# Weight sums laid out one at a time, the gate product on VectorE, and the embedding's rows in the squares' tiles

## The chip, the cores and the metric

The kernel runs on one NeuronCore of one Trainium2 chip. The metric is the device time of one execution in microseconds; the time before is the median of three runs. A profile of one further execution was taken. In it PE is TensorE's matmul (PEld its weight load), DVE is VectorE, ACT is ScalarE, POOL is GpSimd and SP is SyncE, whose queue issues the DMAs.

## The reference

Two layers over 512 tokens of width 1024, float32. Each layer is

```python
h = h + 0.5 * swiglu(rmsnorm(h, ffn1_norm[i]), ffn1_w_gu[i], ffn1_w_down[i])
h = h + mixer(rmsnorm(h, mix_norm[i]))       # layer 0: state-space scan, layer 1: neighbourhood attention
h = h + 0.5 * swiglu(rmsnorm(h, ffn2_norm[i]), ffn2_w_gu[i], ffn2_w_down[i])
gate = sigmoid(rmsnorm(h, ple_norm[i]) @ ple_w_gate[i])
h = h + gate * rmsnorm(p[i] @ ple_w_proj[i], ple_post_norm[i])

def swiglu(x, w_gu, w_down):                 # hidden width 2816 = 22 tiles of 128
    g, u = jnp.split(x @ w_gu, 2, axis=-1)
    return (jax.nn.silu(g) * u) @ w_down
```

The change touches the four `swiglu` (two in each layer) and the product `p[i] @ ple_w_proj[i]`, with `p[i]` 512 x 256 (the embedding's rows).

## The kernel before

**Layout and precision.** The state `h` lies in eight tiles of 128 features x 512 tokens. Every operand of a matmul is split in a high half (a cast) and a low half (the rest). A `gemm` therefore issues three matmuls for each tile of the contraction: high x high (L251), high x low (L254), low x high (L255). For weights the high half `wh` is cast on ACT (L209) and the low half `wl` is subtracted on DVE (L211); for activations these are L269 and L270. There are three buffers each of `wh` and `wl`, four of raw weights `wr`, 24 wide tiles `md`, four tiles `sq` for squares, seven `t`.

**An FFN.** Of the 22 hidden tiles the first six ("plain", `gate_up`) take two units of 24 matmuls each. The other 16 go in eight pairs. In a pair, gate and up rows by halves of the features make a 2 x 2 matrix of weight quadrants `a11`, `a12`, `a21`, `a22`, and the activations one of feature halves by token halves. Their product is formed by seven block products instead of eight (`block`, 24 matmuls 128x256 each, L466 to L468), from sums of quadrants on both sides. The weight sums are `s1 = a21 + a22` (L227), `s2 = s1 - a11` (L228), `a11 - a21` (L229, written over `a21`) and, after block 1, `a12 - s2` (L234). Block 0 uses `a11` as it is, block 1 uses `s2`, block 2 what is in `a21`, block 3 uses `s1`, block 4 `a12`, block 5 the fourth sum, block 6 `a22`. `a21` and `a11` are loaded into `wr`, `a22` and `a12` into `md`.

After a block DVE adds its PSUM to what is kept (L472); ACT copies that of block 0 (L476) and takes silu (L490, L494). After blocks 5 and 6 comes the gate product on POOL (L502), and `halve` splits the result on ACT (L507) and DVE (L508).

**The order.** `ffn_order` lists plain tiles, blocks and downs. A "down" is the down projection of one of the eight `h` tiles over a chunk of hidden tiles: six in the first chunk (18 matmuls), four in the others (12 matmuls). Its result is added on DVE (L527). Downs of the chunk before stand after blocks 0, 2, 4 and 6 of each pair. In the second FFN of a layer `ple_proj` (the product with the embedding's rows, "between") stands ahead of the last chunk's downs. `plan` turns that into a list of steps for weights, which `prep_next` works off at most three units ahead of PE: "u" loads and splits a unit, "g" takes the four quadrants of a pair and issues the three sums, "o" splits a block's operand. `loads` is the order of DMAs on SP's queue. A scheduler then orders the instructions of each engine by what they depend on and by their place in the program, so their order on an engine is not that of the code.

Of the kernel before, what the change touches and what calls it, by code (L numbers as in the profile page):

```python
# [48 lines left out]
def ffn_order():  # L49

    for f in range(PLAIN):
        yield "plain", f
    for c in range(1, len(CHUNKS)):
        a, b = CHUNKS[c]
        blocks = [(p, i) for p in range(a // 2, b // 2) for i in range(7)]
        d = 0
        for n, (p, i) in enumerate(blocks):
            yield "block", p, i  # L60
            while d < KD and (d + 0.5) * len(blocks) <= KD * (n + 1):
                yield "down", c - 1, d
                d += 1
    yield "between",
    for d in range(KD):
        yield "down", len(CHUNKS) - 1, d
# [3 lines left out]
def trunk(ctx, tc, A, out):  # L70
# [72 lines left out]
    def plan():  # L143


        for i in range(stop):
            l, w = divmod(i, 4)
            if w in (0, 2):
                gu, gw, dn = [A[f"w_{x}{1 + w // 2}"][l] for x in ("gu", "gw", "dn")]
                for what, *a in ffn_order():  # L150
                    if what == "plain":
                        for x in range(2):
                            yield "u", gu[a[0], x]
                    elif what == "block":
                        p, i_ = a
                        if i_ == 0:
                            yield "g", [gw[p - PLAIN // 2, x, y] for x, y in ((1, 0), (0, 0), (1, 1), (0, 1))]
                        yield "o", i_
                    elif what == "down":
                        b = CHUNKS[a[0]]  # L160
                        yield "u", dn[a[1], :, b[0] * P:b[1] * P]
                    elif w == 2:
                        for n in range(2):
                            yield "u", A["w_proj"][l, n]
            elif w == 3:
                for n in range(KD):
# [12 lines left out]

    todo = list(plan())  # L180

    loads = [x for what, a in todo if what != "o"
             for x in (zip(a, ("wr", "wr", "md", "md")) if what == "g" else [(a, "wr")])]
    todo = iter(todo)
    raws, ready, splits, blocks = [], [], [], {}
    waiting = {"wr": 0, "md": 0}

    def load_unit():
# [25 lines left out]
    def wide():  # L214
        return md().rearrange("p a b -> p (a b)")

    def prep_next():
        item = next(todo, None)
        if item is None:
            return False  # L220
        what, a = item
        if what == "u":
            split_raw(*take())
        elif what == "g":
            a21, a11, a22, a12 = [take()[0] for _ in range(4)]
            s1, s2 = wide(), wide()
            v.tensor_add(out=s1, in0=a21, in1=a22)  # L227
            v.tensor_sub(out=s2, in0=s1, in1=a11)  # L228
            v.tensor_sub(out=a21, in0=a11, in1=a21)  # L229
            blocks.update({0: a11, 1: s2, 2: a21, 3: s1, 4: a12, 5: s2, 6: a22})  # L230
        else:
            split_raw(blocks[a], 1024)
            if a == 1:
                v.tensor_sub(out=blocks[5], in0=blocks[4], in1=blocks[5])  # L234
        top_up()
        return True

# [118 lines left out]
            return self.ss.end()  # L356


    def ffn(norm, nxt, between=lambda: None, first=None):
        R = [None]  # L360
        mids = {}

# [94 lines left out]
        def block(p, i):  # L457

            pt = mm_bank()
            hi, lo = unit()  # L460
            for j in range(2):
                for kk in range(4):
                    sl = slice((4 * j + kk) * P, (4 * j + kk + 1) * P)
                    o = pt[:, j * HT:(j + 1) * HT]
                    xh, xl = xs[i][kk]
                    te.matmul(out=o, lhsT=hi[:, sl], rhs=xh, start=j == 0 and kk == 0, stop=False)  # L466
                    te.matmul(out=o, lhsT=hi[:, sl], rhs=xl, start=False, stop=False)  # L467
                    te.matmul(out=o, lhsT=lo[:, sl], rhs=xh, start=False, stop=j == 1 and kk == 3)  # L468
            k = kept

            def add(to, other):
                v.tensor_add(out=k[to], in0=pt, in1=k[other])  # L472

            if i == 0:
                k["s"] = t2()
                s.copy(out=k["s"], in_=pt)  # L476
            elif i == 1:
                k["u"] = t2()
                add("u", "s")
            elif i == 2:  # L480
                k["v"] = t2()
                add("v", "u")
            elif i == 3:
                k["w"] = t2()
                add("w", "v")
                add("u", "u")
            elif i == 4:

                add("s", "s")
                s.activation(out=k["s"], in_=k["s"], func=AF.Silu)  # L490
            else:
                if i == 5:
                    add("u", "u")
                    s.activation(out=k["u"], in_=k["u"], func=AF.Silu)  # L494
                    x, gate, c = k["w"], k["u"], slice(HT, T)
                    k["hl"] = md(F32R), md(F32R)
                    for j in range(2):
                        mids[2 * p + j] = tuple(y[:, j, :] for y in k["hl"])
                else:
                    add("v", "v")  # L500
                    x, gate, c = k["v"], k["s"], slice(0, HT)
                g.tensor_mul(out=x, in0=x, in1=gate)  # L502
                halve(k["hl"], x, c)

        def halve(hl, x, c):
# [5 lines left out]
        for what, *a in ffn_order():  # L511
            if what == "plain":
                gate_up(a[0])
                while left and R[0] is not None:
                    sums(left.pop(0))
                    if a[0] < 4:
                        break
            elif what == "block":
                block(*a)
            elif what == "between":  # L520
                made = between()
            else:
                c, d = a
                last = c == len(CHUNKS) - 1
                pt = mm_bank() if last else px_bank()
                gemm(pt, unit(), [mids[f] for f in range(*CHUNKS[c])])
                v.scalar_tensor_tensor(out=h[d], in0=pt, scalar=0.5, in1=h[d], op0=ALU.mult, op1=ALU.add)  # L527
                if last:
                    nxt(d)
                    if d == 2 and made is not None:  # L530
                        made[1]()
# [1 line left out]


    def ple_proj(l):
        pt_ = xa(F32)
        sy.dma_start(out=pt_, in_=A["p"][l])
        prs = []
        for k in range(2):
            pr = xa()  # L540
            split(pr, pt_[:, k, :], None)
            prs.append(pr)
        ss = SumSq()
        pp = []
# [12 lines left out]

        def finish():
            r3 = ss.rsqrt(4.0, 4.0 * EPS)
            for n in range(KD):  # L560
                pp[n] = (pp[n], r3)

        return pp, finish

    def ple(l, norm, pp, nxt):
        halves = (slice(0, T // 2), slice(T // 2, T))
# [697 lines left out]
    for i in range(stop):  # L1264
        l, w = divmod(i, 4)
        last = i == stop - 1
        m = None if last else Norm(gains[i + 1], (lambda: md(F32R)) if w == 2 else xa)
        nxt = done if last else m.prep
        if w == 0:
            ffn(n, nxt, first=first if i == 0 else None)  # L1270
        elif w == 1:
            (ssd if l % 2 == 0 else attention)(n, nxt)
        elif w == 2:
            pp = ffn(n, nxt, lambda: ple_proj(l))
        else:
            ple(l, n, pp, nxt)
        n = m
# [99 lines left out]
```

## Time and profile before

| | us |
|---|---|
| median of three runs | 2443.38 (2441.11 to 2443.71) |
| profiled execution, device time | 2437.86 |
| its span in the trace | 2436.1 |
| PE busy | 2354.6 (97%) |
| DVE busy | 1799.9 (74%) |
| ACT busy | 1107.4 (45%) |
| POOL busy | 481.0 (20%) |

The mean granted clock of TensorE was 0.99 of full speed. A row of a group reads: line, engine, operation, output <- inputs, shapes, count, then busy us and mean ns of one, then the idle time of the engine just before them and what ended it. A row of a timeline reads: start, duration (us), engine, line, operation, and in brackets the idle time before it with its releaser. The pairs of the four FFNs lie at about 77 to 360, 1006 to 1285, 1440 to 1722 and 2062 to 2346 us.

### The profile page before, as it was taken

The numbers are of one execution on the slowest core, as the hardware profiler recorded it, in microseconds if no ns is written. First come the engines' busy times: TensorE is split into PE (matmuls) and PEld (weight loads), VectorE is DVE, ScalarE is ACT, GpSimd is POOL, SyncE is SP. The second block draws the span as 40 slices with busy tenths as digits, with TensorE's granted clock in tenths as the row PEclk, the third lists the DMA queues.
The fourth block names the chain that finished last, engine by engine and source line by source line (L and its number), as shares of the span: only waits on it lengthen the run. The fifth ranks groups of instructions, "written<-read, shape, count | busy, mean of one in ns | idle before, by whom it ended". The sixth has DMA issues, their size and how long they took to land. (4 is left out here: it accounts for less than half of the span.)

```text
span 2436.1 us, 35198 instructions
## 1 busy us (share of the span) xinstructions
PE 2354.6 (97%) x13810; PEld 2036.8 (84%) x13810; DVE 1799.9 (74%) x2501; ACT 1107.4 (45%) x1819; POOL 481.0 (20%) x373
## 2 busy tenths in 40 slices
PE   9999999999999999999999999999999999999998
PEld 8888888888888888888887888888877888988887
DVE  7777768877777757877676887677678758677757
ACT  5433335655556744433335443333437644333343
POOL 1101111344545631111103211011100011011120
PEclk9999999999999999999999999999999999999999
DMA  5223314544444543332223232222442323333222
GB/s 184 91 88 104 100 53 139 174 136 143 142 141 130 166 150 96 102 106 89 93 70 104 87 118 91 96 83 74 147 134 100 113 84 116 92 95 100 68 81 85
DMA packets 98950, 265.95 MB, mean 109 GB/s; under 512 B 11984, under 2 KB 12880, under 8 KB 98784
## 3 DMA queue, kind: packets, MB, share of 16 engines
q1 hardware_dynamic: 98496, 263.57, 33.8%
q8 instruction: 108, 1.77, 0.3%
q14 instruction: 58, 0.48, 0.1%
q10 hardware_dynamic: 288, 0.14, 0.0%
HBM read 253.40 MB, written 10.26 MB: 108 GB/s over the span
## 5 line engine op out<-in xcount | busy, mean ns | idle before, releaser
L255 PE MATMUL ps<-md,wl 128*128 128x512 f32 x2128 | 841.7, 396 | 56.7 <-DVE wl L211 56.7
L251 PE MATMUL ps<-md,wh 128*128 128x512 f32 x2128 | 846.7, 399 | 8.5 <-ACT md L269 8.0
L254 PE MATMUL ps<-md,wh 128*128 128x512 f32 x2128 | 838.5, 394 | 2.3 <-DVE md L270 1.6
L209 ACT CAST wh<-wr 128x1024 fp32r<-128x1024 f32 (+2 forms) x401 | 357.6, 893 | 454.8 <-PE ps L254 210.6
L255 PEld LDWEIGHTS ps<-md,wl 128*128 128x128 f32 x2128 | 404.4, 190 | 155.4 <-DVE wl L211 70.6
L211 DVE TENSOR_TENSOR wl<-wr,wh 128x1024 fp32r<-128x1024 f32 (+2 forms) x401 | 427.9, 1067 | 116.4 <-ACT wh L209 90.9
L251 PEld LDWEIGHTS ps<-md,wh 128*128 128x128 f32 x2128 | 404.9, 190 | 91.8 <-ACT md L269 10.0
L254 PEld LDWEIGHTS ps<-md,wh 128*128 128x128 f32 x2128 | 405.1, 190 | 85.3 <-issue 3.3
L502 POOL TENSOR_TENSOR t<-t,t 128x512 f32<-128x512 f32 x64 | 124.3, 1942 | 974.0 <-ACT t L494 876.3
L209 ACT CAST wh<-md 128x1024 fp32r<-128x1024 f32 x160 | 167.4, 1046 | 275.0 <-PE ps L467 263.3
L472 DVE TENSOR_TENSOR t<-ps,t 128x512 f32<-128x512 f32 x224 | 151.7, 689 | 157.5 <-PE ps L468 157.5
L468 PE MATMUL ps<-sc,wl 128*128 128x256 f32 x896 | 254.0, 284 | 2.2 <-DVE wl L211 2.2
L466 PE MATMUL ps<-sc,wh 128*128 128x256 f32 x896 | 253.8, 283 | 1.6 <-ACT wh L209 1.6
L467 PE MATMUL ps<-sc,wh 128*128 128x256 f32 x896 | 254.0, 284 | 0.0
L468 PE MATMUL ps<-md,wl 128*128 128x256 f32 x896 | 253.6, 283 | 0.0
L467 PE MATMUL ps<-md,wh 128*128 128x256 f32 x896 | 253.5, 283 | 0.0
L466 PE MATMUL ps<-md,wh 128*128 128x256 f32 x896 | 253.4, 283 | 0.0
L211 DVE TENSOR_TENSOR wl<-md,wh 128x1024 fp32r<-128x1024 f32 x160 | 195.2, 1220 | 25.7 <-ACT wh L209 25.7
L297 POOL TENSOR_TENSOR sq<-sq,sq 128x512 f32<-128x512 f32 x71 | 100.9, 1421 | 425.9 <-ACT sq L293 425.1
L466 PEld LDWEIGHTS ps<-sc,wh 128*128 128x128 f32 x896 | 172.4, 192 | 6.0 <-ACT wh L209 2.0
L467 PEld LDWEIGHTS ps<-sc,wh 128*128 128x128 f32 x896 | 172.2, 192 | 3.9
L468 PEld LDWEIGHTS ps<-sc,wl 128*128 128x128 f32 x896 | 172.1, 192 | 2.4 <-DVE wl L211 2.4
(207 smaller groups left out, 3024.2 us busy)
## 6 DMA issues: line engine op xcount, KB each, us to landing
wr<-in_w_in_dram SPq DMA_DIRECT2D x65, 512.0 KB, 3.6
wr<-in_w_gw_dram SPq DMA_DIRECT2D x64, 512.0 KB, 3.5
md<-in_w_gw_dram SPq DMA_DIRECT2D x64, 512.0 KB, 5.2
wr<-in_w_dn_dram SPq DMA_DIRECT2D x128, 256.0 KB, 2.7
wr<-in_w_gu_dram SPq DMA_DIRECT2D x44, 512.0 KB, 3.4
hs<-crow SPq DMA_DIRECT2D x64, 256.0 KB, 3.9
wr<-in_w_dn_dram SPq DMA_DIRECT2D x32, 384.0 KB, 3.2
wr<-in_w_qkv_dram SPq DMA_DIRECT2D x24, 512.0 KB, 3.6
```

Source lines behind the costliest of these rows:

```text
L209: splits.append(s.copy(out=hi[:, :n], in_=raw[:, :n]))
L211: v.tensor_sub(out=lo[:, :n], in0=raw[:, :n], in1=hi[:, :n])
L251: m = te.matmul(out=pt, lhsT=hi[:, sl], rhs=part(xp, 0, cols), start=first and k == 0, stop=False)
L254: te.matmul(out=pt, lhsT=hi[:, sl], rhs=part(xp, 1, cols), start=False, stop=False)
L255: te.matmul(out=pt, lhsT=lo[:, sl], rhs=part(xp, 0, cols), start=False, stop=last and k == n - 1)
L297: (v if fast else g).tensor_add(out=self.acc, in0=self.acc, in1=q)
L466: te.matmul(out=o, lhsT=hi[:, sl], rhs=xh, start=j == 0 and kk == 0, stop=False)
L467: te.matmul(out=o, lhsT=hi[:, sl], rhs=xl, start=False, stop=False)
L468: te.matmul(out=o, lhsT=lo[:, sl], rhs=xh, start=False, stop=j == 1 and kk == 3)
L472: v.tensor_add(out=k[to], in0=pt, in1=k[other])
L502: g.tensor_mul(out=x, in0=x, in1=gate)
```

## The change

Three things, each seen in the diff:

1. The step "g" only takes the quadrants. The three sums become steps "s" of their own. They and the group's loads are listed beside blocks 4, 5 and 6 of the pair before (for the first pair: beside the last three plain units). What the blocks use is kept for each pair.
2. The gate product is issued on `v` (DVE) and not on `g` (POOL).
3. The embedding's rows are loaded by two DMAs of 256 KB into two `sq` tiles ahead of the last chunk's first block, and not by one of 512 KB into an `md` tile at "between"; `ple_proj` becomes a generator for that.

```diff
+                def ahead(p, i_):
+                    if i_ == 0:
+                        yield "g", [gw[p - PLAIN // 2, x, y] for x, y in ((1, 0), (0, 0), (1, 1), (0, 1))]
+                    yield "s", (p, i_)
+
                 for what, *a in ffn_order():
                     if what == "plain":
                         for x in range(2):
                             yield "u", gu[a[0], x]
+                            n = 2 * a[0] + x - (2 * PLAIN - 3)
+                            if n >= 0:
+                                yield from ahead(PLAIN // 2, n)
                     elif what == "block":
-                        p, i_ = a
-                        if i_ == 0:
-                            yield "g", [gw[p - PLAIN // 2, x, y] for x, y in ((1, 0), (0, 0), (1, 1), (0, 1))]
-                        yield "o", i_
+                        yield "o", a
+                        if a[1] >= 4 and a[0] < NF // 2 - 1:
+                            yield from ahead(a[0] + 1, a[1] - 4)
...
         elif what == "g":
-            a21, a11, a22, a12 = [take()[0] for _ in range(4)]
-            s1, s2 = wide(), wide()
-            v.tensor_add(out=s1, in0=a21, in1=a22)
-            v.tensor_sub(out=s2, in0=s1, in1=a11)
-            v.tensor_sub(out=a21, in0=a11, in1=a21)
-            blocks.update({0: a11, 1: s2, 2: a21, 3: s1, 4: a12, 5: s2, 6: a22})
+            group[:] = [take()[0] for _ in range(4)]
+        elif what == "s":
+            p, i = a
+            a21, a11, a22, a12 = group
+            if i == 0:
+                blocks[p] = {0: a11, 2: a21, 3: wide(), 4: a12, 6: a22}
+                v.tensor_add(out=blocks[p][3], in0=a21, in1=a22)
+            elif i == 1:
+                blocks[p][1] = blocks[p][5] = wide()
+                v.tensor_sub(out=blocks[p][1], in0=blocks[p][3], in1=a11)
+            else:
+                v.tensor_sub(out=a21, in0=a11, in1=a21)
...
-                g.tensor_mul(out=x, in0=x, in1=gate)
+                v.tensor_mul(out=x, in0=x, in1=gate)
...
     def ple_proj(l):
-        pt_ = xa(F32)
-        sy.dma_start(out=pt_, in_=A["p"][l])
+        pt_ = [sq() for _ in range(2)]
+        for k in range(2):
+            sy.dma_start(out=pt_[k], in_=A["p"][l, :, k])
+        yield
         prs = []
         for k in range(2):
             pr = xa()
-            split(pr, pt_[:, k, :], None)
+            split(pr, pt_[k], None)
             prs.append(pr)
```

In the changed kernel the lines have other numbers. In the pieces of its order below L220 is the low half of a weight (L211 before), L240, L243 and L245 are the three sums (L227 to L229), L251 is the fourth sum (L234), L489 is the addition (L472), L519 the gate product, L525 and L524 the halving (L508 and L507), L546 the down's addition (L527), L218 the cast of a weight (L209), L286 and L287 the split of an activation (L269 and L270), L468 is L451 and L462 to L465 are L445 to L448. Tile names carry running numbers, so a number in one kernel is another tile in the other.

DVE at a boundary of two pairs in the first FFN, before. The first row is the low half for block 0 (`a11`, 128x1024), the two halvings are of the pair before, the first 128x512 low half is that of the down after block 0, and the last row is the low half for block 1:

```order
L211 TENSOR_TENSOR wl_1706<-wr_1574,wh_1704 128x1024
L508 TENSOR_TENSOR md_1690<-t_1604,md_1689 128x2x256
L227 TENSOR_TENSOR md_1695<-wr_1492,md_1576 128x1024
L472 TENSOR_TENSOR t_1549<-ps_1694,t_1549 128x512
L228 TENSOR_TENSOR md_1696<-md_1695,wr_1574 128x1024
L229 TENSOR_TENSOR wr_1492<-wr_1574,wr_1492 128x1024
L508 TENSOR_TENSOR md_1690<-t_1549,md_1689 128x2x256
L211 TENSOR_TENSOR wl_1739<-wr_1661,wh_1737 128x512
L527 SCALAR_TENSOR_TENSOR hs_81<-ps_1736,hs_81 128x512
L211 TENSOR_TENSOR wl_1759<-md_1696,wh_1757 128x1024
```

The same boundary on DVE, of the changed kernel, from block 0's low half to the low half for block 2 and the sums behind it:

```order
L220 TENSOR_TENSOR wl_1706<-wr_1416,wh_1704 128x1024
L519 TENSOR_TENSOR t_1610<-t_1610,t_1522 128x512
L489 TENSOR_TENSOR t_1553<-ps_1703,t_1553 128x512
L220 TENSOR_TENSOR wl_1739<-wr_1576,wh_1737 128x512
L525 TENSOR_TENSOR md_1699<-t_1610,md_1698 128x2x256
L519 TENSOR_TENSOR t_1553<-t_1553,t_1471 128x512
L546 SCALAR_TENSOR_TENSOR hs_81<-ps_1736,hs_81 128x512
L220 TENSOR_TENSOR wl_1763<-md_1645,wh_1761 128x1024
L525 TENSOR_TENSOR md_1699<-t_1553,md_1698 128x2x256
L251 TENSOR_TENSOR md_1645<-md_1420,md_1645 128x1024
L240 TENSOR_TENSOR md_1897<-wr_1670,md_1743 128x1024
L220 TENSOR_TENSOR wl_1795<-wr_1345,wh_1793 128x1024
```

The three sums that stood between the low halves of block 0 and of the down are gone from there; the sums of the pair after (the first is L240 here, the others follow after block 2's low half) stand behind block 1's, and the gate products stand among the rest.

DVE at the first pair of the first FFN, before; the first L211 is block 0's low half, the second that of the first down (128x768):

```order
L447 TENSOR_TENSOR t_663<-t_654,t_663 128x256
L211 TENSOR_TENSOR wl_686<-wr_559,wh_684 128x1024
L448 TENSOR_TENSOR t_664<-t_654,t_663 128x256
L451 TENSOR_TENSOR md_661<-t_663,md_661 128x512
L227 TENSOR_TENSOR md_675<-wr_495,md_561 128x1024
L451 TENSOR_TENSOR md_662<-t_664,md_662 128x512
L228 TENSOR_TENSOR md_676<-md_675,wr_559 128x1024
L229 TENSOR_TENSOR wr_495<-wr_559,wr_495 128x1024
L211 TENSOR_TENSOR wl_714<-wr_593,wh_712 128x768
```

The same place of the changed kernel:

```order
L464 TENSOR_TENSOR t_671<-t_662,t_671 128x256
L245 TENSOR_TENSOR wr_374<-wr_465,wr_374 128x1024
L465 TENSOR_TENSOR t_672<-t_662,t_671 128x256
L468 TENSOR_TENSOR md_669<-t_671,md_669 128x512
L220 TENSOR_TENSOR wl_686<-wr_465,wh_684 128x1024
L468 TENSOR_TENSOR md_670<-t_672,md_670 128x512
L220 TENSOR_TENSOR wl_714<-wr_561,wh_712 128x768
```

The third sum, one L465 and one L468 now stand ahead of block 0's low half, and the first two sums stand further up (between the sums of the activations of the plain tiles before), where there were none.

ACT ahead of the product with the embedding's rows, before; the last two rows cast the two halves of the rows, and `wh_11938` is the projection's second unit:

```order
L494 ACTIVATE t_11730<-t_11730 128x512
L507 CAST md_11897<-t_11812 128x2x256
L209 CAST wh_11938<-wr_11786 128x1024
L507 CAST md_11897<-t_11761 128x2x256
L209 CAST wh_11965<-wr_11869 128x512
L269 CAST md_11959<-md_11957 128x512
L269 CAST md_11962<-md_11957 128x512
```

The same of the changed kernel:

```order
L511 ACTIVATE t_11734<-t_11734 128x512
L218 CAST wh_11942<-wr_11790 128x1024
L524 CAST md_11901<-t_11816 128x2x256
L524 CAST md_11901<-t_11765 128x2x256
L218 CAST wh_11967<-wr_11873 128x512
L286 CAST md_11961<-sq_11334 128x512
L286 CAST md_11964<-sq_11335 128x512
```

The casts of the rows stay behind both halvings and the next down's cast; the inputs are now the two `sq` tiles, and the unit's cast has moved ahead of the first halving. On PE the order of the matmuls is the same but for a few at the first pair of an FFN.

More of the change, by code (lines that the diff above doesn't have):

```diff
@@ L180, in trunk @@
     todo = list(plan())
-    loads = [x for what, a in todo if what != "o"
+    loads = [x for what, a in todo if what in "gu"
              for x in (zip(a, ("wr", "wr", "md", "md")) if what == "g" else [(a, "wr")])]
     todo = iter(todo)
-    raws, ready, splits, blocks = [], [], [], {}
+    raws, ready, splits, group, blocks = [], [], [], [], {}
     waiting = {"wr": 0, "md": 0}
@@ L224, in prep_next @@
         elif what == "g":
-            a21, a11, a22, a12 = [take()[0] for _ in range(4)]
-            s1, s2 = wide(), wide()
-            v.tensor_add(out=s1, in0=a21, in1=a22)
-            v.tensor_sub(out=s2, in0=s1, in1=a11)
-            v.tensor_sub(out=a21, in0=a11, in1=a21)
-            blocks.update({0: a11, 1: s2, 2: a21, 3: s1, 4: a12, 5: s2, 6: a22})
-        else:
-            split_raw(blocks[a], 1024)
-            if a == 1:
-                v.tensor_sub(out=blocks[5], in0=blocks[4], in1=blocks[5])
+            group[:] = [take()[0] for _ in range(4)]
[10 more added lines that the diff above has]
+                v.tensor_sub(out=a21, in0=a11, in1=a21)
+        else:
+            p, i = a
+            b = blocks[p]
+            split_raw(b[i], 1024)
+            if i == 1:
+                v.tensor_sub(out=b[5], in0=b[4], in1=b[5])
         top_up()
@@ L356, in end, with ffn @@
             return self.ss.end()
-    def ffn(norm, nxt, between=lambda: None, first=None):
+    def ffn(norm, nxt, between=None, first=None):
         R = [None]
@@ L518, in ffn @@
             elif what == "block":
+                if between and a == [CHUNKS[-1][0] // 2, 0]:
+                    next(between)
                 block(*a)
             elif what == "between":
-                made = between()
+                made = between and next(between)
             else:
@@ L561, in finish @@
                 pp[n] = (pp[n], r3)
-        return pp, finish
+        yield pp, finish
     def ple(l, norm, pp, nxt):
@@ L1273, in trunk @@
         elif w == 2:
-            pp = ffn(n, nxt, lambda: ple_proj(l))
+            pp = ffn(n, nxt, ple_proj(l))
         else:
```

## The prediction

> **What bounds the kernel now.** I read the page's first part, then its groups, then PE's timeline and the other engines' round the longest idle times.
>
> ```profile
> PE 2354.6 (97%) x13810; PEld 2036.8 (84%) x13810; DVE 1799.9 (74%) x2501; ACT 1107.4 (45%) x1819; POOL 481.0 (20%) x373
> L255 PE MATMUL ps<-md,wl 128*128 128x512 f32 x2128 | 841.7, 396 | 56.7 <-DVE wl L211 56.7
> md<-in_w_gw_dram SPq DMA_DIRECT2D x64, 512.0 KB, 5.2
> ```
>
> TensorE is the bound, so only its idle and its slow time can be won. Nearly all its idle time, 56.7 us, stands in one group: the third matmul of a gemm, waiting for a weight's low half `wl` (L211). The same group asked for in the windows of the first and the last of the four FFNs (the two between also read 12.9):
>
> ```profile
> L255 PE MATMUL ps<-md,wl 128*128 128x512 f32 x130 | 52.1, 401 | 12.9 <-DVE wl L211 12.9
> L255 PE MATMUL ps<-md,wl 128*128 128x512 f32 x130 | 53.4, 410 | 12.9 <-DVE wl L211 12.9
> ```
>
> So 4 x 12.9 = 51.6 us lie in the seven boundaries between pairs of each FFN. One of these boundaries, on PE and on DVE, POOL and ACT (start, duration, in us):
>
> ```profile
> 258.48 0.28 PE L468 MATMUL ps<-md,wl 128*128 128x256 f32 x1
> 258.60 0.40 PE L251 MATMUL ps<-md,wh 128*128 128x512 f32 x1
> 258.83 0.40 PE L254 MATMUL ps<-md,wh 128*128 128x512 f32 x1
> 261.43 0.50 PE L255 MATMUL ps<-md,wl 128*128 128x512 f32 x1 [2.19 <-DVE wl L211]
> ```
> ```profile
> 251.30 1.23 DVE L211 TENSOR_TENSOR wl<-wr,wh 128x1024 fp32r<-128x1024 f32 x1 [0.31 <-ACT wh L209]
> ...
> 254.98 1.22 DVE L227 TENSOR_TENSOR md<-wr,md 128x1024 f32<-128x1024 f32 x1
> 256.11 0.69 DVE L472 TENSOR_TENSOR t<-ps,t 128x512 f32<-128x512 f32 x1
> 256.71 1.22 DVE L228 TENSOR_TENSOR md<-md,wr 128x1024 f32<-128x1024 f32 x1
> 257.85 2.32 DVE L229 TENSOR_TENSOR wr<-wr,wr 128x1024 f32<-128x1024 f32 x1
> 260.09 0.68 DVE L508 TENSOR_TENSOR md<-t,md 128x512 fp32r<-128x512 f32 x1
> 260.69 0.68 DVE L211 TENSOR_TENSOR wl<-wr,wh 128x512 fp32r<-128x512 f32 x1
> ```
> ```profile
> 256.88 2.20 POOL L502 TENSOR_TENSOR t<-t,t 128x512 f32<-128x512 f32 x1 [3.19 <-DVE t L472]
> 259.11 0.62 ACT L507 CAST md<-t 128x512 fp32r<-128x512 f32 x1 [4.25 <-POOL t L502]
> ```
>
> The down after block 0 starts at 258.60 and needs its low half for its third matmul; DVE makes it at 260.69. Ahead of it stand the three sums of the next pair (L227 to L229) and a halving (L508) that comes after POOL's gate product. L229 lasts 2.32 there instead of the 1.22 of its neighbour; POOL's product runs from 256.88 to 259.08, over its first half. From 258.83 to 261.43 are 2.60 us where 258.60 to 258.83 took 0.23: a stall costs 2.37, that is 0.18 above its idle. Two forms of a pair follow, one period each (columns: time, then busy time of PE, PEld, DVE, ACT, POOL, then granted clock):
>
> ```profile
> 227.82:261.43 33.61, 31.41 (x217) 29.08 (x217) 24.89 (x29) 12.32 (x17) 3.94 (x2) 1.00 0.31 95
> 295.02:330.19 35.17, 32.97 (x216) 30.28 (x217) 24.97 (x29) 12.31 (x17) 3.94 (x2) 0.95 0.20 61
> 295.00:298.50 3.50, 3.48 (x8) 2.80 (x9) 3.50 (x4) 0.71 (x2) 0.00 (x0) 0.51 0.48 142
> ```
>
> After some stalls the clock stands near one half for about 3.4 us, and the pair takes 1.57 longer. By the windows of all pairs that is so after 8 of the 28 stalls, and the eight stretches begin within 1.5 us of a stall's end.
>
> **The change, part by part, and the sum.**
>
> *Sums one at a time, and the gate product on VectorE (go together).* The order shows that the three sums leave their place between block 0's low half and the down's. They stand now one pair earlier, among the low halves of blocks 1 and 2. What stands between block 0's low half and the down's is one gate product and one addition. From 251.30 + 1.13 (254.98 to 256.11, what a 1024-wide operation occupies) = 252.43: product 0.60 (256.11 to 256.71, what a 512-wide one occupies), addition 0.60 when the block's PSUM is done, so the down's low half is written by about 254.5, 4 us before 258.83. Then follow two halvings, the other product, a down's addition, block 1's low half, the pair's own fourth sum (L234) and the next pair's first sum at about 259.75; block 2's low half follows at about 260.9 and is written at 262.05. Block 1 follows the down: PE reaches it at 258.60 + 12 x 0.23 = 261.35 and block 2 at 261.35 + 24 x 0.12 (258.48 to 258.60) = 264.2, so block 2's low half has 2.2 us to spare. None of this stalls PE. DVE's load in a pair is 24.89 - 1.1 (L229 without POOL beside it) + 2 x 0.60 = 25.0, in a period of 33.61 - 2.37 = 31.24: 80%, so DVE stays under PE. Gain: 51.6 + 28 x 0.18 (5.0) = 56.6, of which I take 56.3, since the first two stalls of an FFN are the short ones.
>
> *The half clock after stalls.* With no stall there is nothing for it to follow: 8 x 1.57 = 12.6 gained.
>
> The Trainium skill speaks against this term: "TensorE: Matmul & The Clock Gate", section "HAM oscillation — how this bites in real kernels", says that idle gaps above about 3.4 us throttle, and a 2.19 us gap is shorter; Part 1 says that the window runs freely. By it the stretches would have another cause and would stay, and the sum would be 12.6 smaller. In this trace they all follow stalls, which is why I keep the term.
>
> *First pair of the first FFN.* Here DVE is full, and the sums move ahead of block 0's low half:
>
> ```profile
> 77.19 0.39 PE L468 MATMUL ps<-sc,wl 128*128 128x256 f32 x1 [2.20 <-DVE wl L211]
> 82.15 0.39 PE L466 MATMUL ps<-sc,wh 128*128 128x256 f32 x1 [1.59 <-ACT wh L209]
> 83.00 0.50 PE L255 MATMUL ps<-md,wl 128*128 128x512 f32 x1 [0.34 <-DVE wl L211]
> ```
> ```profile
> 75.92 1.22 DVE L211 TENSOR_TENSOR wl<-wr,wh 128x1024 fp32r<-128x1024 f32 x1
> 77.05 0.42 DVE L448 TENSOR_TENSOR t<-t,t 128x256 f32<-128x256 f32 x1
> 77.39 0.68 DVE L451 TENSOR_TENSOR md<-t,md 128x512 fp32r<-128x512 f32 x1
> 77.99 1.22 DVE L227 TENSOR_TENSOR md<-wr,md 128x1024 f32<-128x1024 f32 x1
> ```
> ```profile
> 83.40:86.80 3.40, 3.40 (x10) 2.63 (x9) 3.02 (x4) 0.85 (x2) 2.47 (x1) 0.50 0.94 287
> ```
>
> By the order, three sums, one L448 and one L451 come ahead of that low half: 75.92 + 3 x 1.13 + 0.34 + 0.60 = 80.25, written at 81.5. PE can do some four other matmuls first and is then idle for some 6 us instead of 2.20; the two later waits go, since the sums are then done; a half clock follows as before. I take a loss of 2.5, between 1 (the later waits pay for nearly all) and 5 (a second half-clock stretch of 3.40, costing 1.7, and none paid).
>
> *The same place in the other three FFNs.* There DVE has more room:
>
> ```profile
> 1012.72 0.50 PE L254 MATMUL ps<-md,wh 128*128 128x512 f32 x1 [0.53 <-DVE md L270]
> 1000.46 1.22 DVE L211 TENSOR_TENSOR wl<-wr,wh 128x1024 fp32r<-128x1024 f32 x1
> ```
>
> With the same 4.33 us ahead of it, block 0's low half starts at 1004.8 and is written at 1006.0. The stalled matmul is the 17th of the down after block 0, so that block starts 0.7 + 16 x 0.23 + 2.87 earlier, at about 1005.5, and wants it 0.24 later. That is 0.3 late at most if DVE can start nothing earlier, and in time if it can; I hold 0 to 0.6 each. The wait at 1012.72 (there are three such, 0.53 + 0.18 each) goes, as the sums no longer stand ahead of that split. I take +0.5 each, 1.5.
>
> *The embedding's rows.* Loaded early, they are no part of the wait. What that wait is now:
>
> ```profile
> 1286.60 2.07 PE L251 MATMUL ps<-md,wh 128*128 128x512 f32 x4 [3.77 <-ACT md L269]
> 2345.65 1.41 PE L251 MATMUL ps<-md,wh 128*128 128x512 f32 x4 [3.77 <-ACT md L269]
> 1282.69 2.17 POOL L502 TENSOR_TENSOR t<-t,t 128x512 f32<-128x512 f32 x1 [2.06 <-DVE t L472]
> 1284.89 0.62 ACT L507 CAST md<-t 128x512 fp32r<-128x512 f32 x1 [2.66 <-POOL t L502]
> 1285.00:1291.70 6.70, 5.10 (x12) 4.00 (x13) 3.10 (x5) 2.89 (x6) 0.00 (x0) 0.50 0.24 73
> ```
>
> The split's cast stands on ACT behind L507, which waits for POOL's product. On DVE this product is done at about 1281.3, and the cast can start when the next down's cast is through, at about 1283.2. PE's first matmul comes at about 1283.8, its first low-half operand at 1284.9. Each place costs 3.95 and some 2.3 of half clock now (5.1 us of matmuls at half speed, the second place less): 12.5 in all. After: 2.1 and some 0.5 each, 5.2. Gain 7.3. The two loads cost SP two issues at the FFN's start instead of one; nothing is late behind them in the order, so 0, between 0 and 0.5.
>
> *The ends of the first FFN of each layer.*
>
> ```profile
> 359.88 0.51 PE L251 MATMUL ps<-md,wh 128*128 128x512 f32 x1 [0.27 <-ACT md L507]
> 360.61 0.50 PE L254 MATMUL ps<-md,wh 128*128 128x512 f32 x1 [0.22 <-DVE md L508]
> ```
>
> With the product earlier by more than that, 0.27 + 0.22 + 2 x 0.18 = 0.85 go, twice: 1.7.
>
> The sum: 56.3 + 12.6 - 2.5 + 1.5 + 7.3 + 1.7 = 76.9. The profiled execution took 2437.86, so it would take 2361. The median of the runs shown, 2443.38, is 5.5 above it; I take most of that along and say 2365.
>
> **Rivals.**
>
> *The wait only moves.* DVE at 80% has its work in lumps: the sums stand now before the low halves of blocks 1 and 2, and products, halvings and additions before the down's. If one of them is late by 0.5 to 1.0 in each of 28 pairs, 14 to 28 come back: 2379 to 2393. For it: three operations in a row behind a late PSUM are 1.8 to 3.4 us, as large as the 2.2 us to spare. Against it: the 4 us before the down. Of the pairs after, PE would then show idle before L468, from `wl`.
>
> *The half clock stays.* Of 28 stalls of one length only eight bring it, so something besides the stall decides, and it may come without one: 2365 + 12.6 = 2378. Against it: all eight begin at a stall, none between. The Trainium skill's rule on gaps, cited above, would give this time.
>
> *Slower: the first sum waits for its load.* L227 now stands in DVE's order ahead of block 2's low half and needs two blocks of the next pair, one pair earlier than before. Their issue has to wait until block 0's split frees a raw buffer (252.43), and 5.2 later, at about 257.7, they are there: 2.0 before DVE wants them, and another 2.2 pass before PE notices. Each us beyond costs 28 us, so the gain of 76.9 is eaten when PE waits 2.75 in each pair: when a load takes over 5.2 + 2.0 + 2.2 + 2.75 = 12.1 us. The page's median for these loads is 5.2. 3 in 100.
>
> *The change does nothing:* the waits come from PE's or ACT's order and not from what stands ahead on DVE. Against it stand the rows at 260.09 and 260.69, back to back. 2443, 2 in 100.
>
> **How the numbers follow.** The gain as summed: 0.70, with its own range 2352 to 2376 (the loss at the first pair 1 or 5, the other places 0 or 0.6 each, the 5.5 not taken along or in full, one or two half clocks). The wait moves: 0.17. The half clock stays: 0.08. Slower: 0.03; nothing: 0.02. The range 2350 to 2393 leaves out the last two and a tail on either side. A measurement of this kernel tells about 0.2% (4.9 us) from no change; faster by more than that 0.95, within it 0.02, slower 0.03.
>
> **What would show it.** Right: the group L255 with under 6 us of idle, pairs of 31.2 us at clock 1.00, the sum L229 at 1.22 throughout, about 25.0 us of DVE in a pair; a longer idle time, about 6 us, at 76 to 82 us in the first FFN; about 2 us of idle before the first matmuls of the embedding. Wrong: idle before L466 or L468 from `wl` or `wh` in each pair (the wait moved), DVE idle before L227 with a DMA as its end (the load), or a clock of 0.95 in pairs without a stall.

## The result, and the profile after

The changed kernel takes 2353.1 us, the median of 4 runs (2351.47 to 2353.81), against 2442.61 us for the kernel before in the same comparison. The ratio is 0.9633, with a 95% interval from 0.9616 to 0.965. So it is 89.5 us faster; the forecast was 2365, with a range from 2350 to 2393. The profiled execution took 2352.96 (span 2351.2). One execution of the kernel before, in a later comparison, took 12038 us at a granted clock of 0.178; the ratios, differences and ranges here are of the others.

The same parts of the page as before, of the changed kernel (L272 is L255 before, L268 is L251):

```profile
PE 2327.4 (99%) x13810; PEld 2026.6 (86%) x13810; DVE 1805.7 (77%) x2565; ACT 1111.8 (47%) x1819; POOL 353.7 (15%) x309
L268 PE MATMUL ps<-md,wh 128*128 128x512 f32 x2128 | 838.4, 395 | 2.7 <-ACT md L286 2.1
L272 PE MATMUL ps<-md,wl 128*128 128x512 f32 x2128 | 830.7, 391 | 4.7 <-DVE wl L220 4.7
```

The idle time of the group that waited for a weight's low half has fallen from 56.7 to 4.7 us, and PE is busy for 99% of the span. Two pairs of the first FFN and one of the second, as windows (time, busy time of PE, PEld, DVE, ACT, POOL, granted clock), and the third sum's group on DVE:

```profile
190.45:221.57 31.12, 31.12 (x217) 29.16 (x216) 24.98 (x31) 12.41 (x17) 0.00 (x0) 1.00 0.30 94
221.57:252.69 31.12, 31.12 (x217) 29.15 (x216) 24.98 (x31) 12.42 (x17) 0.00 (x0) 1.00 0.32 108
1159.45:1190.58 31.13, 31.13 (x218) 29.16 (x217) 24.99 (x31) 12.44 (x17) 0.00 (x0) 1.00 0.30 101
```
```profile
L245 DVE TENSOR_TENSOR wr<-wr,wr 128x1024 f32<-128x1024 f32 x32 | 39.0, 1218 | 0.0
```

A pair takes 31.12 us, where it took 33.61 or 35.17. PE is busy throughout and DVE carries 24.98 us; the clock is 1.00 in every pair but the first of the first FFN (below). The sum L245 (L229 before) is back at 1.22 us. DVE at the boundary at 252.69:

```profile
244.92 1.23 DVE L220 TENSOR_TENSOR wl<-wr,wh 128x1024 fp32r<-128x1024 f32 x1 [0.31 <-ACT wh L218]
...
247.41 0.68 DVE L220 TENSOR_TENSOR wl<-wr,wh 128x512 fp32r<-128x512 f32 x1
...
253.34 1.22 DVE L240 TENSOR_TENSOR md<-wr,md 128x1024 f32<-128x1024 f32 x1
254.48 1.22 DVE L220 TENSOR_TENSOR wl<-wr,wh 128x1024 fp32r<-128x1024 f32 x1
```

The down's low half (247.41) is written at 248.09, 4.6 us before PE's third matmul of the down starts at 252.69.

Taking the same matmul in both traces and subtracting its times shows where 84.9 us between the two profiled executions lie:

| part | gained, us | forecast |
|---|---|---|
| 28 boundaries of pairs, with the half clock behind them | 72.2 | 68.9 |
| first pair of the first FFN | -1.0 | -2.5 |
| first pair of the other three FFNs | 2.7 | 1.5 |
| embedding, two places | 9.4 | 7.3 |
| ends of the first FFNs | 1.9 | 1.7 |

The rest, -0.3, is small changes of either sign elsewhere. The rows at the first pair of the first FFN and at the embedding:

```profile
79.94 0.58 PE L483 MATMUL ps<-sc,wh 128*128 128x256 f32 x1 [4.19 <-ACT wh L218]
81.55 0.58 PE L485 MATMUL ps<-sc,wl 128*128 128x256 f32 x1 [0.82 <-DVE wl L220]
```
```profile
79.60:86.40 6.80, 5.64 (x24) 5.35 (x25) 5.70 (x8) 1.44 (x3) 2.03 (x1) 0.50 0.50 136
```
```profile
1250.68 1.42 PE L268 MATMUL ps<-md,wh 128*128 128x512 f32 x5 [1.05 <-ACT md L286]
```

PE now waits 4.19 and 0.82 at the first pair and then runs 6.8 us at half clock; the waits at 82.15 and 83.00 are gone. At the embedding 1.05 us of idle is left of 3.77, with no half clock behind it; at the second embedding it is 1.05 as well. PE's order differs from that of before at these two places too (16 matmuls at each), and not only at the first pair of an FFN.

### The profile page after: what moved, and what is told of

Its sections match the earlier page's. It is cut to its first block, busy times and chain, and to the rows that moved or that the text cites. A ratio compares the mean times of both kernels' runs of the same rounds, so it can differ in the third digit from the quotient of the medians.

```text
span 2351.2 us, 35169 instructions
## 1 busy us (share of the span) xinstructions
PE 2327.4 (99%) x13810; PEld 2026.6 (86%) x13810; DVE 1805.7 (77%) x2565; ACT 1111.8 (47%) x1819; POOL 353.7 (15%) x309
## 3 DMA queue, kind: packets, MB, share of 16 engines
q8 instruction: 108, 1.77, 0.3%
## 4 chain that ended last, share of the span: by engine, by line
PE 90%; DVE 5%; ACT 1%; issue 1%; POOL 1%; DMA 1%; SPq 0%; POOLq 0%; ACTq 0%; DVEq 0%
PE ps L268 19%; PE ps L271 19%; PE ps L272 19%; PE ps L485 9%; PE ps L484 9%; PE ps L483 9%; PE ps L866 1%; DVE wl L220 1%; PE ps L844 1%; PE ps L887 1%; PE ps L800 1%; PE ps L786 1%; PE ps L1172 1%; DVE md L290 1%; DVE md L287 1%
## 5 line engine op out<-in xcount | busy, mean ns | idle before, releaser
L268 PE MATMUL ps<-md,wh 128*128 128x512 f32 x2128 | 838.4, 395 | 2.7 <-ACT md L286 2.1
L272 PE MATMUL ps<-md,wl 128*128 128x512 f32 x2128 | 830.7, 391 | 4.7 <-DVE wl L220 4.7
L218 ACT CAST wh<-wr 128x1024 fp32r<-128x1024 f32 (+2 forms) x401 | 358.1, 894 | 521.4 <-PE ps L271 199.9
L220 DVE TENSOR_TENSOR wl<-wr,wh 128x1024 fp32r<-128x1024 f32 (+2 forms) x401 | 429.0, 1070 | 114.1 <-ACT wh L218 85.3
L272 PEld LDWEIGHTS ps<-md,wl 128*128 128x128 f32 x2128 | 400.1, 188 | 90.7 <-DVE wl L220 6.7
L268 PEld LDWEIGHTS ps<-md,wh 128*128 128x128 f32 x2128 | 400.5, 188 | 84.4 <-issue 3.5
L271 PEld LDWEIGHTS ps<-md,wh 128*128 128x128 f32 x2128 | 400.9, 188 | 81.1 <-issue 3.3
L218 ACT CAST wh<-md 128x1024 fp32r<-128x1024 f32 x160 | 167.7, 1048 | 297.8 <-PE ps L484 263.0
L489 DVE TENSOR_TENSOR t<-ps,t 128x512 f32<-128x512 f32 x224 | 151.7, 689 | 129.8 <-PE ps L485 127.9
L220 DVE TENSOR_TENSOR wl<-md,wh 128x1024 fp32r<-128x1024 f32 x160 | 196.5, 1228 | 26.8 <-ACT wh L218 26.7
L484 PEld LDWEIGHTS ps<-md,wh 128*128 128x128 f32 x896 | 172.4, 192 | 1.2
L483 PEld LDWEIGHTS ps<-md,wh 128*128 128x128 f32 x896 | 172.4, 192 | 1.2
```

Of the source, the lines that this page charges most:

```text
L218: splits.append(s.copy(out=hi[:, :n], in_=raw[:, :n]))
L220: v.tensor_sub(out=lo[:, :n], in0=raw[:, :n], in1=hi[:, :n])
L268: m = te.matmul(out=pt, lhsT=hi[:, sl], rhs=part(xp, 0, cols), start=first and k == 0, stop=False)
L271: te.matmul(out=pt, lhsT=hi[:, sl], rhs=part(xp, 1, cols), start=False, stop=False)
L272: te.matmul(out=pt, lhsT=lo[:, sl], rhs=part(xp, 0, cols), start=False, stop=last and k == n - 1)
```

## The experiments

Each kernel ran in rounds beside the kernel before.

| run | what differs | median, us | ratio to before (95%) |
|---|---|---|---|
| e1_product | before + product on VectorE | 2360.7 | 0.967 (0.9655 to 0.9684) |
| x2_sums_only | before + sums ahead | 2363.9 | 0.9683 (0.9666 to 0.97) |
| e3_rows | before + embedding's rows early | 2432.3 | 0.9961 (0.9949 to 0.9973) |
| e2_sums | all but the product | 2357.3 | 0.9657 (0.9641 to 0.9673) |
| e4_no_rows | all but the rows | 2357.0 | 0.9655 (0.9641 to 0.967) |
| x1_sums_later | before, sums after block 0's down | 2403.1 | 0.9838 (0.9822 to 0.9854) |
| x6_one_sum_ahead | before + third sum ahead | 2380.8 | 0.975 (0.9735 to 0.9765) |
| after_again | the change | 2352.5 | 0.964 (0.9627 to 0.9654) |
| f4_first_pair | the change, first pair's sums later | 2352.5 | 0.9639 (0.9626 to 0.9653) |
| f6_first_pair_b | the same, another place | 2353.3 | 0.9641 (0.9628 to 0.9654) |

**The product alone.**

```diff
-                g.tensor_mul(out=x, in0=x, in1=gate)
+                v.tensor_mul(out=x, in0=x, in1=gate)
```

> The kernel before, with the gate product on VectorE alone; sums and embedding's rows as before. Theory S (the sums must leave their place): the three sums still come in one lump at the pair's boundary, so only the stretch of L229 (1.1 us) goes from each of 28 stalls, with the half clock behind them: about 2443 - 28 x 1.1 - 12.6 - 9.4 (embedding) - 1.9 (ends of the first FFNs) = 2388, with idle of about 1.1 us left in the group L255 per boundary. Theory O (what stands ahead of the down's low half decides, and the scheduler sets that): with the product on VectorE the order puts the down's low half ahead of the sums; block 1's low half then comes at about 261.4 where block 1 wants it at 261.6, so the stalls go too: 2355 to 2360, less than 0.4 us idle per boundary. The waits at the first pair of the three later FFNs (L254 from L270, 0.8 each) stay under both.

Measured: 2360.7, so 81 us come with this one word. Theory S falls; theory O's range is missed by 0.7. DVE at a boundary of this kernel:

```profile
245.35 1.23 DVE L211 TENSOR_TENSOR wl<-wr,wh 128x1024 fp32r<-128x1024 f32 x1 [0.31 <-ACT wh L209]
246.49 0.69 DVE L502 TENSOR_TENSOR t<-t,t 128x512 f32<-128x512 f32 x1
247.22 0.69 DVE L472 TENSOR_TENSOR t<-ps,t 128x512 f32<-128x512 f32 x1
247.83 0.68 DVE L211 TENSOR_TENSOR wl<-wr,wh 128x512 fp32r<-128x512 f32 x1
248.43 0.69 DVE L508 TENSOR_TENSOR md<-t,md 128x512 fp32r<-128x512 f32 x1
249.03 1.22 DVE L227 TENSOR_TENSOR md<-wr,md 128x1024 f32<-128x1024 f32 x1
...
251.91 1.22 DVE L229 TENSOR_TENSOR wr<-wr,wr 128x1024 f32<-128x1024 f32 x1
```

In the kernel before, the first halving of the pair (L508) follows the low half of 251.30 only after a wait, which goes back over ACT to POOL's product:

```profile
251.95 1.74 POOL L502 TENSOR_TENSOR t<-t,t 128x512 f32<-128x512 f32 x1 [26.47 <-ACT t L494]
253.72 0.62 ACT L507 CAST md<-t 128x512 fp32r<-128x512 f32 x1 [1.91 <-POOL t L502]
254.37 0.69 DVE L508 TENSOR_TENSOR md<-t,md 128x512 fp32r<-128x512 f32 x1 [1.84 <-ACT md L507]
```

With the product on DVE the sums are still in the boundary (L227 to L229), but the down's low half (247.83) now stands ahead of them, these 1.84 us of waiting are gone, and L229 takes 1.22. The group L255 is left with 5.1 us of idle in the whole kernel:

```profile
L255 PE MATMUL ps<-md,wl 128*128 128x512 f32 x2128 | 832.2, 391 | 5.1 <-DVE wl L211 5.1
```

**The sums alone,** first with the rows early, then without (the change of `plan` as above; `g.tensor_mul` kept).

> The changed kernel with the gate product back on GpSimd; sums ahead and embedding's rows early as in the change. Theory S: the stalls at the boundaries go (56 us) and the half clock behind them; what the product on GpSimd holds up stays: the embedding's two waits with their half clock (9.4) and the ends of the first FFNs (1.9), so 2353 + 11.3 = 2364. Theory P (the product on GpSimd is the cause, by its time and by stretching VectorE's sums): the stalls stay at about 2.4 per boundary, about 2430. In between: block 2's low half comes at about 264.5 where it is wanted at 264.45, so up to 0.3 per pair may show as idle before L485, 8 us in all: 2372.

> The kernel before with the sums one at a time beside the pair before, product on GpSimd and rows as before: the first part of the change alone. If the parts for the embedding add up: 2357.3 (sums and rows) + 9.6 (what the rows alone gave) = 2367, with no stall at the boundaries and the embedding's wait of 3.8 us and its half clock as before. Rival: the rows matter less once the sums are moved: 2358 to 2362.

Measured: 2357.3 and 2363.9. Theory P falls as well: the stalls go with the product still on POOL. The first time is 7 us under theory S, which had kept the whole loss at the embedding; the second lies between the two forecasts. In the run with the rows early a pair takes the same 31.12 us, with POOL's two products in it:

```profile
190.45:221.57 31.12, 31.12 (x218) 29.16 (x217) 23.41 (x29) 12.33 (x17) 3.40 (x2) 1.00 0.30 92
```

So either edit is enough at the boundaries. By the same matmuls in two profiles, the boundaries and the half clock behind them give 72.0 us with the product alone, 72.2 with the sums alone and 72.2 with the whole change. Over the whole kernel it is 81 us with the product, 78 with the sums, and 85 with both (the run without rows). The gains do not add up, since both edits remove the same overrun.

**One sum ahead.** From the kernel with the sums alone, `ahead` yields only `("s", (p, 2))`, into a tile of its own; the other two stay at block 0.

> As the run with the sums only, but only the third difference (a11 - a21, to a tile of its own) is made ahead; s1 and s2 stay at block 0 of their own pair. Theory B (a margin that is overrun): two sums fit between block 0's low half and the down's, the down's low half comes at about 258.5 where it is wanted at 259.0, block 1's at 261.7 against 261.6, so nearly all of the stall goes with this one sum: 2367 to 2373, under 0.3 us idle per boundary. Rival (proportional: each sum carries a third of the stall): 2.36 falls by 1.1, no half clock, 2442 - 31 - 17 = 2394.

Measured: 2380.8, between the two. The boundary in PE, DVE and POOL:

```profile
255.60 0.51 PE L276 MATMUL ps<-md,wl 128*128 128x512 f32 x1 [0.46 <-DVE wl L223]
```
```profile
252.63 1.21 DVE L246 TENSOR_TENSOR md<-md,wr 128x1024 f32<-128x1024 f32 x1
253.76 1.78 DVE L223 TENSOR_TENSOR wl<-wr,wh 128x512 fp32r<-128x512 f32 x1
```
```profile
252.79 2.20 POOL L523 TENSOR_TENSOR t<-t,t 128x512 f32<-128x512 f32 x1 [3.19 <-DVE t L493]
```

Of 2.19 us of idle 0.46 is left. Without the third sum the low half itself (253.76, usually 0.68) is what runs into POOL's product, takes 1.78 and ends 0.55 after it: theory B had left out this 1.1. A third of the sums thus takes away over three quarters of this idle time and all of the half clock, which is nearer to an overrun of a margin than to a price for each sum.

**The sums after the down.**

```diff
...
+                        if i_ == 1:
+                            yield "s", p
                         yield "o", i_
...
```

> The kernel before, with the three sums as one lump listed after the down that follows block 0, just ahead of block 1's operand; product on GpSimd and rows as before. On VectorE the down's low half then stands ahead of all sums. Theory A (what counts is only what stands ahead of the down's low half): the boundary's stall goes, about 2442 - 56 - 17 = 2370. Theory B (VectorE has more to do between a block's low half and block 1's than the time there allows, as long as the second halving waits for the product on GpSimd): sums, second halving, a down's addition and the cast of block 1's operand end at about 263.7 where block 1 wants it at 261.6, so the stall moves to block 1 (L466 from wh or L468 from wl) with about 2 us each: 2425 to 2445.

Measured: 2403.1, under what theory B gave and above what A gave. The wait did move to block 1, as B has it, but is shorter:

```profile
257.13 0.38 PE L471 MATMUL ps<-sc,wh 128*128 128x256 f32 x1 [0.53 <-ACT wh L211]
258.39 0.38 PE L473 MATMUL ps<-sc,wl 128*128 128x256 f32 x1 [0.76 <-DVE wl L213]
```
```profile
251.27 2.31 DVE L232 TENSOR_TENSOR md<-wr,md 128x1024 f32<-128x1024 f32 x1
```
```profile
224.19:257.13 32.94, 31.65 (x217) 29.14 (x217) 24.87 (x29) 12.32 (x17) 3.40 (x2) 1.00 0.30 97
```

The pair takes 32.94 us: two waits of 0.53 and 0.76. Now the first sum (L232) is the one beside POOL's product, at 2.31. Where the sums stand thus decides which operation waits; in these runs they fit only with fewer of them there, or with no wait for POOL. The clock stays 1.00 in these pairs. By the same matmuls the boundaries take 34.9 us less than before: 12.6 for the eight half clocks, and 22.3 for shorter waits (33.60 to 32.94 in a pair, and none at the first two boundaries of an FFN).

**The embedding's rows.** The kernel before with two `sq` tiles and the generator, and the changed kernel with the old load.

> The kernel before with the embedding's rows alone loaded early into the squares' tiles; sums and product as before. My theory: the rows were in place before their cast could start, which stands on ScalarE behind the halving of a product on GpSimd; the wait of 3.8 us at the embedding stays and the time is that of the kernel before within 1 us. Rival: the load is what the wait ends with: the two waits shrink by up to 2 us each with their half clock, 2437 at the least.

> The changed kernel with the embedding's rows loaded as before (one DMA of 512 KB when the product with them is reached). The product on VectorE has the cast ready 3 us earlier, so the load may now be last: issued some 2.8 us before the cast wants it, landing 3.7 after its issue: 0.9 lost at each of two places and half a chance of a half clock (1.6): 2354 to 2358. Rival: hidden, 2353, the wait at the embedding stays 1.05 us from ACT md L286.

Measured: 2432.3 against 2441.94, so the kernel with the rows alone is 9.6 us faster (6.6 to 12.5 by the interval), and my theory falls. Not all of this is the embedding. The stalls of the boundaries are still there, and the half clocks behind them differ from execution to execution: the ten executions range from 2424.1 to 2436.8, and the profiled one took 2436.8, with 11 half clocks in the pairs where the profile of before has eight. In the changed kernel the rows are worth 3.9 (2357.0 against 2353.1, from different comparisons). What the two places of the embedding give by the same matmuls, their own half clocks included, in us against before:

| | product on POOL | product on DVE |
|---|---|---|
| sums and rows as before | 0 | 3.4 (e1_product) |
| sums as before, rows early | 7.3 (e3_rows) | not run |
| sums ahead, rows as before | 1.3 (x2_sums_only) | 4.7 (e4_no_rows) |
| sums ahead, rows early | 7.3 (e2_sums) | 9.4 (the change) |

So the rows give more there than the product, with either order of the two. ACT and PE at the embedding, of the kernel before with the rows early:

```profile
1287.20 0.62 ACT L507 CAST md<-t 128x512 fp32r<-128x512 f32 x1 [1.91 <-POOL t L502]
1287.73 0.62 ACT L269 CAST md<-sq 128x512 fp32r<-128x512 f32 x1
1288.25 1.04 ACT L209 CAST wh<-wr 128x1024 fp32r<-128x1024 f32 x1
1289.20 0.61 ACT L269 CAST md<-sq 128x512 fp32r<-128x512 f32 x1
1290.93 0.62 ACT L507 CAST md<-t 128x512 fp32r<-128x512 f32 x1 [1.12 <-POOL t L502]
```
```profile
1289.81 0.50 PE L254 MATMUL ps<-md,wh 128*128 128x512 f32 x1 [0.20 <-DVE md L270]
1293.84 0.50 PE L254 MATMUL ps<-md,wh 128*128 128x512 f32 x1 [1.70 <-DVE md L270]
```

The rows' casts (L269) now stand ahead of the second halving, which waits for POOL. In the kernel before they stood behind it, and the trace put the wait down to that halving. With nothing changed but the load, the order on ACT is another; that the scheduler had laid it out round the late load is inferred. In the changed kernel ACT's order is the same with and without early rows, and without them the load itself ends last:

```profile
1249.57 1.14 ACT L286 CAST md<-md 128x512 fp32r<-128x512 f32 x2 [0.26 <-DMA md<-in_p_dram]
```

**The first pair of the first FFN.** The change, but there with s1 and s2 listed after the down behind block 0 (f4) or right behind block 0's operand (f6), the third sum after block 1:

```diff
...
+                        late = i == 0 and a[0] == PLAIN // 2
+                        if late and a[1] == 1:
+                            yield from [("s", (a[0], 0)), ("s", (a[0], 1))]
                         yield "o", a
+                        if late and a[1] == 1:
+                            yield "s", (a[0], 2)
...
```

The piece is that of f4.

> The changed kernel once more, for comparison on the same chip with the two runs after it: 2353 within 2.

> The changed kernel, but for the first pair of the first FFN the sums are listed after the down that follows block 0 (s1, s2) and after block 1 (the third), so that block 0's low half is not behind them there. VectorE works without a gap in this stretch, so the work only changes its order: the wait before block 0 falls from 4.4 to 2.4, while block 1's low half comes some 2 us late instead: idle 4.5 in place of 6.0, and one half clock or none in place of 6.8 us of it. 2349 to 2352. Rival: the same time, since VectorE's backlog sets the end of this stretch: 2353.

> As the last, but s1 and s2 listed right behind block 0's operand. The down's low half comes at about 81.7 where it is wanted at 80.5, block 1's in time: waits of 2.4, 1.2 and 0.5 against 6.0 in the changed kernel, and one half clock at most: 2349 to 2351. Rival as before: 2353.

Measured: 2352.5, 2352.5 and 2353.3, no difference; the rival stands. The longest waits of f4:

```profile
77.57 0.39 PE L492 MATMUL ps<-sc,wl 128*128 128x256 f32 x1 [2.18 <-DVE wl L226]
87.04 0.39 PE L490 MATMUL ps<-sc,wh 128*128 128x256 f32 x1 [0.97 <-ACT wh L224]
88.18 0.38 PE L490 MATMUL ps<-sc,wh 128*128 128x256 f32 x1 [0.63 <-ACT wh L224]
```

By the same matmuls, PE is 3.9 us ahead of the changed kernel where that stands at 84 us, and level again at 100 us. This fits the rival, by which DVE's backlog sets the end of the stretch; a run with less work on DVE there was not made. Neither order beats the change.

## Why the prediction was right

*The boundaries.* The step held: no stall at any of the 28, DVE at 24.98 us a pair (25.0 forecast), the down's low half early. The order came as drawn: the first sum starts 8.42 us after block 0's low half (8.45 forecast). The wait did not move either: in the pairs PE's only idle times over 0.15 us are the two at the first pair. With the half clock the term was 3.3 us too small: a pair is 2.48 shorter (33.60 to 31.12) and not 2.37. What the prediction did not see is that sums and product, which it priced together, each do this alone. The overrun had several causes in one row: 1.84 us of DVE waiting for the halving behind POOL, 1.1 of L229 behind POOL's product, and 3.4 of sums. Taking away the first two with the product, or the third, brings the low half in time; one sum of three left 0.46 us of idle.

*The half clock.* It went with the stalls, in all pairs but the first of the first FFN, where a wait is left. The rival that it stays, and with it the Trainium skill's rule on gaps ("TensorE: Matmul & The Clock Gate", section "HAM oscillation — how this bites in real kernels"), is refuted here: stalls of 2.19 us of idle brought it and the change removed it.

*The embedding.* The wait fell to 1.05 us of idle where 2.1 in all was forecast, without half clock: 9.4 gained and not 7.3. The attribution was wrong: the whole 7.3 was put down to the product, and the rows' early load was costed at 0. At the two places the product alone gives 3.4, the rows alone 7.3, and beside the rest the rows give about half of the 9.4. That the term came near is therefore luck. The step that failed is "loaded early, they are no part of the wait": I read the order of ACT as given, and it changed with the load; and with the product on DVE the late load would itself have ended the wait.

*The first pairs.* The wait of about 6 us in the first FFN came as 4.19 + 0.82 of idle and two half-clock windows in place of one; net -1.0 against -2.5. In the other FFNs nothing is lost, 0.9 gained each.

*The carry-over to the median.* 5.5 us between the profiled execution and the median of before were taken along in good part (4 of them). After the change the two agree (2352.96 and 2353.1). The 5 us belonged to before: its executions range from 2437.3 to 2444.4 over the comparisons, and the last section has a likely reason. The sum was 8.0 short, this step another 4; together they are the distance to 2365.

*The load for the first sum* (the rival on the slow side) shows in DVE's groups with 0.3 us of idle in 32 sums:

```profile
L240 DVE TENSOR_TENSOR md<-wr,md 128x1024 f32<-128x1024 f32 x32 | 39.0, 1217 | 0.3 <-DMA md<-in_w_gw_dram 0.3
```

## What to carry to other kernels

A stall behind a queue of work on another engine can be an overrun of a margin: list all that stands between the last on-time operation and the late one, waits too. Removing one large item may then end it, and the gains of two such edits do not add up. Price each part of a change alone before pricing them together. Where a scheduler sets the order, an earlier operand or a moved operation can change the order itself, so a releaser read from the trace of before is no proof that another input is free. Where half clocks come and go between executions, compare the same matmuls in two traces, place by place, before giving a difference of medians to an edit.

## What the runs showed of the hardware

**The half clock follows a fixed grid of windows.** In each of the twelve profiles all half-clock stretches after the first 60 us begin on one grid of 3.413 us (to 0.004 us; in the kernel before those at 83.42, 295.04 and 1185.92 us lie 62 and 261 windows apart). Which windows are halved goes with PE's idle time within the window before. Windows of the grid in the kernel before, each with its successor:

```profile
257.50:260.91 3.41, 1.73 (x13) 1.29 (x11) 3.41 (x4) 1.80 (x3) 1.58 (x1) 1.00 0.00 0
260.91:264.32 3.41, 2.90 (x15) 2.48 (x16) 3.41 (x5) 1.68 (x3) 0.00 (x0) 1.00 0.60 155
...
291.63:295.04 3.41, 1.22 (x10) 0.78 (x8) 3.41 (x4) 2.33 (x3) 1.05 (x1) 1.00 0.10 8
295.04:298.45 3.41, 3.41 (x8) 2.73 (x9) 3.41 (x4) 0.67 (x2) 0.00 (x0) 0.50 0.48 145
```

The two stalls have the same length. One is cut by the window's end, with PE busy for 1.73 us in the window; the other lies whole in its window, with 1.22. Only the second is followed by a half clock. Over all twelve profiles, 60 windows at full clock were followed by a half clock. PE was idle for 1.88 us or more in 58 of them, and for 1.63 and 1.77 us in the other two. Of the 106 windows with over 0.9 us of idle that were not followed by one, none had more than 1.87 us. So a stall with 2.19 us of idle brings a half clock in about 54% of the places in which it can lie to the grid, if 1.88 us are needed in one window (an estimate: (1.22 + 2 x 0.31) / 3.41, from 3.41 - 2.19 and 2.19 - 1.88). That is some 11 of the 20 long stalls (five in each FFN; the first two there are of 1.1 and 0.8 us); the profile of before had 8, and that of e3_rows, with the same stalls, 11. At 1.57 each, three more are 4.7 us, which is the distance of the profiled execution of before to its median. That this is the cause of the distance fits the granted clocks (0.990 there, mostly 0.988 or 0.989 in the longer runs) but was not tested by itself. The Trainium skill, "TensorE: Matmul & The Clock Gate", section "Part 1: The HAM clock gate (the "warmup" mystery)", has this free window of 3413 ns, and the traces agree. That a gap has to be longer than 3.4 us, as the section cited above says, is what they do not bear out.

**A VectorE operation on two SBUF tiles that starts beside POOL's product waited for its end.** L229 before ended at 260.17, 1.09 after POOL's product (259.08), and lasted 2.32; at all 28 boundaries it took 2.31 or 2.32. The low half in x6 ended at 255.54, 0.55 after the product there (254.99), and lasted 1.78. L228, begun 0.17 before the product, kept its 1.22. Two operations with one input from PSUM that start beside another product of POOL (L401 and L398 at 41.82 and 42.41, the product from 41.45 to 42.76) took their usual 0.68. It is thus the operation's place in time that decides which one pays. One case went the other way: a weight's low half that starts at 85.20, beside a product begun at 84.33, kept its 1.22, and there the product took 3.23. The Trainium skill, "SBUF — State Buffer", section "Who interferes with whom", describes an exclusive hold of a port pair by whoever issues first; these rows agree with it.
